# Squares of the last attention's queries on ScalarE, and the moving operands of the products at 64 bytes past multiples of 512

## The chip, the core and the metric

The kernel runs as one program on one core of a Trainium2 chip. The core has five engines that run side by side and meet through semaphores: TensorE (PE in the profile; its weight loads are shown as PEld), VectorE (DVE), ScalarE (ACT), GpSimd (POOL) and SyncE (SP), which issues the DMAs here. The metric is the time of one execution on the device in microseconds, from start to end. On-chip memory (SBUF) has 128 partitions; an address in it, below, is the byte offset of a tile inside each partition, the same in all of them.

## What is computed

The reference runs three transformer blocks on one sequence of 256 tokens and 1024 channels, all in float32. Cut to what matters:

```
x = first_block(x, mem, ...)        # norm, gated mixing + forgetting attention + memory attention, norm, relu^2 FFN
for i in range(2):                  # second block, two layers
    x = x + 0.5 * swiglu(rmsnorm(x, ffn_norm1[i]), wg1, wu1, wd1)   # 1024 -> 2816 -> 1024
    h = rmsnorm(x, mix_norm[i])
    x = x + (sliding_window_attention if i == 0 else latent_attention)(h, ...)
    x = x + 0.5 * swiglu(rmsnorm(x, ffn_norm2[i]), wg2, wu2, wd2)

def latent_attention(h, ...):       # the last attention: 16 heads of 64 + 32 channels
    c_q, c_kv, k_rope = split(h @ w_in)
    q = (rmsnorm(c_q) @ w_uq).reshape(16 heads, 96)
    k, v = from rmsnorm(c_kv) @ w_ukv, k_rope shared by all heads
    q, k = rmsnorm(q) * q_gain, rmsnorm(k) * k_gain      # over the 96 channels of a head
    q, k = rotate the last 32 channels by position
    o = softmax(causal(q k^T / sqrt(96))) v ;  return o @ w_out
```

The norm of a query needs the sum of the squares of its 96 channels; those squares are the first subject of the change.

## The kernel before

**Products.** Activations lie with channels on the partitions and the 256 tokens along the free axis: `x`, and its two parts `xh` and `xl`, are eight tiles of 128 x 256 floats each (1024 bytes per partition). Each float32 product is made of three: value and weight are split into a rounded float32r part and the rest (`h`, `lo`), and `mm_t` (lines 129 to 137) issues for each 128 channels the three matmuls weight-h by value-h (L135), weight-h by value-l (L136) and weight-l by value-h (L137). In `mm_t` the 128 x 128 piece of weights is the stationary operand, and the 128 x 256 activation tile is the one that moves through the array. So each of these matmuls streams 256 columns of an activation tile. `mm_n` (L145 to L147) and `mm_y` (L159 to L161) do it the other way round: activations stationary, weights moving.

The activation tiles that move in `mm_t` are `xh`, `xl` (the normalised residual; gate and up products and most projections), `ah`, `al` (the inner values of the four SwiGLU layers, for the down products), `oh`, `ol` (the attention's output, for its output projection) and `mh`, `ml` (the memory).

**Weights.** They come in as `raw` chunks by DMA from SP's queue, three chunks ahead. ScalarE casts each part to `wh` (L103), VectorE takes the difference to `wl` (L113), six parts deep and four ahead of the products (`Stream`).

**Where tiles lie.** Pools are placed one after another in the order in which they are opened (`lead`, `wp`, `lead2`, `res`, `tp`, `cst`, `sm`, then the pools of each stage), and each tile takes its size rounded up to 32 bytes. A tile without a use therefore moves all that comes behind it. `lead2` begins with one such tile of 8 floats, `fill` (line 172). The addresses of the built program, as remainders by 512 bytes, are:

```
operand                         remainder by 512 bytes
xh, xl  (pool res)              0
ah, al, oh, ol, mh, ml, ch, cl  480   (pools of the stages, behind sm)
wh, wl  (pool wp)               224   (every 128-column piece too)
```

**The last attention.** Queries come in four groups of four heads (`q_mm(0)` to `q_mm(3)`), each as two halves of 128 tokens in the tiles `qn[0]`, `qn[1]`. `q_sq(b)` squares group b into two tiles `qsq` of 128 x 384: group 0 on ScalarE (L1225), groups 1 to 3 on GpSimd (L1223). `q_norm(b)` sums them on VectorE (L1229) and takes the power -1/2 on GpSimd (L198); `q_rope(b)` rotates the last 32 channels (L1240, L1243, L1245), groups 0 and 1 on VectorE, 2 and 3 on GpSimd. `head(h)` transposes a head's keys and queries on TensorE (L1268, L1270) and copies them to `kT` and `qT` (L1273, L1274).

The heads then go through a software pipeline: each `pipe.step()` issues the scores of a new head (L311), the masked maximum and the negated bound of it on VectorE (L1255, L1260), the exponential on ScalarE (L281), the scaling of the head before by its sum on VectorE (L299), the transposes of the one before that (L322, copied by L325) and the products with the values (L343). The code runs under a manual schedule: every engine executes its instructions in the order in which the Python code issues them. So the order of the calls at the end of that stage (`q_mm(1)`, `q_norm(0)`, `head(0, act)`, ...) is the order on each engine, and an instruction that waits holds up all behind it on its engine.

## Time and profile before

| | |
|---|---|
| median of 3 runs | 1250.59 us (1250.11 to 1250.6) |
| the profiled execution: time | 1250.49 us |
| its span, first to last instruction | 1248.7 us |
| mean granted TensorE clock | 0.993 of full speed |
| PE busy / DVE / ACT / POOL | 98% / 67% / 53% / 14% |
| matmuls | 9850 |

A matmul's shown duration (0.28 us for 256 columns) overlaps that of the next: they are pipelined, and a new one starts every 0.12 us or so. What a matmul costs is this distance from start to start, which the timeline shows, and which a stretch of nothing but such matmuls gives as its length by their number. A row of the view by windows counts every matmul that touches the window, so also the two or three that were running when it began.

### The profile page before, as it was taken

To read this page: it belongs to the slowest core of one execution; us is meant where nothing else is said; L and a number is where in the kernel's file an instruction comes from. 1 tells how busy PE (TensorE), PEld (TensorE's weight loads), DVE (VectorE), ACT (ScalarE), POOL (GpSimd) and SP (SyncE) were. 2 spreads that over 40 slices of the span, in tenths; PEclk is the share of its full clock that TensorE was granted. 3 is DMA by queue.
4 is the path that set the end of the run, shared out by engine and by line. 5 is a ranking of instruction groups with operands and counts; after the bars stand their busy time and mean duration, and the time that the engine had idled before them with its cause. 6 is when DMAs were issued, how large, how long until landed. Compare 5 with 4: busy or idle time off the path is not lost.

```text
span 1248.7 us, 23875 instructions
## 1 busy us (share of the span) xinstructions
PE 1222.7 (98%) x9850; PEld 1169.1 (94%) x9850; DVE 836.3 (67%) x1470; ACT 658.8 (53%) x1164; POOL 171.6 (14%) x168
## 2 busy tenths in 40 slices
PE   8998999999999999999999999999999899999998
PEld 6886999888999999988999999999999779999998
DVE  5867776844688666797666666676666797566653
ACT  5574655443554444587454444444444787454532
POOL 5404100300301001212000011000011552000000
PEclk9999999999999999999999999999999989999999
DMA  7543354655254545623455456455455413455462
GB/s 242 200 141 120 130 208 174 234 204 196 75 203 169 181 147 184 233 102 111 168 195 188 143 185 228 173 187 196 146 186 198 169 36 124 161 189 197 137 212 97
DMA packets 37262, 211.31 MB, mean 169 GB/s; under 512 B 4768, under 2 KB 8224, under 8 KB 18848
## 3 DMA queue, kind: packets, MB, share of 16 engines
q1 hardware_dynamic: 37152, 209.78, 48.4%
q8 instruction: 77, 1.26, 0.4%
q14 instruction: 33, 0.27, 0.1%
HBM read 208.71 MB, written 1.05 MB: 168 GB/s over the span
## 4 chain that ended last, share of the span: by engine, by line
PE 84%; DVE 10%; ACT 3%; issue 1%; DMA 1%; POOL 1%; SPq 0%; ACTq 0%; DVEq 0%; POOLq 0%
PE ps L135 23%; PE ps L136 23%; PE ps L137 23%; DVE wl L113 4%; PE ps L161 3%; PE ps L159 3%; PE ps L160 3%; PE ps L343 1%; PE ps L311 1%; PE ps L145 1%; PE ps L147 1%; PE ps L322 1%; PE ps L146 1%; ACT wh L103 1%; DVE p L299 1%
## 5 line engine op out<-in xcount | busy, mean ns | idle before, releaser
L113 DVE TENSOR_TENSOR wl<-raw,wh 128x1024 fp32r<-128x1024 f32 (+4 forms) x436 | 493.0, 1170 | 54.5 <-ACT wh L103 54.2
L135 PE MATMUL ps<-xh,wh 128*128 128x256 f32 (+1 forms) x1848 | 519.9, 281 | 2.2 <-DVE y L527 1.7
L137 PE MATMUL ps<-xh,wl 128*128 128x256 f32 (+1 forms) x1848 | 516.2, 279 | 1.3 <-DVE wl L113 1.3
L136 PE MATMUL ps<-xl,wh 128*128 128x256 f32 (+1 forms) x1848 | 515.9, 279 | 0.3 <-DVE xl L271 0.3
L103 ACT CAST wh<-raw 128x1024 fp32r<-128x1024 f32 (+4 forms) x436 | 400.8, 958 | 94.0 <-PE ps L160 33.9
L135 PEld LDWEIGHTS ps<-xh,wh 128*128 128x128 f32 (+1 forms) x1848 | 346.7, 188 | 5.0 <-ACT sq L208 2.1
L137 PEld LDWEIGHTS ps<-xh,wl 128*128 128x128 f32 (+1 forms) x1848 | 346.6, 188 | 1.8 <-DVE wl L113 1.7
L136 PEld LDWEIGHTS ps<-xl,wh 128*128 128x128 f32 (+1 forms) x1848 | 346.8, 188 | 0.7 <-DVE xl L271 0.5
L135 PE MATMUL ps<-ah,wh 128*128 128x256 f32 x704 | 199.2, 283 | 0.0
L136 PE MATMUL ps<-al,wh 128*128 128x256 f32 x704 | 199.2, 283 | 0.0
L137 PE MATMUL ps<-ah,wl 128*128 128x256 f32 x704 | 199.2, 283 | 0.0
L409 ACT ACTIVATE s<-t 128x256 f32<-128x256 f32 x88 | 36.9, 420 | 187.5 <-DVE t L407 187.5
L137 PEld LDWEIGHTS ps<-ah,wl 128*128 128x128 f32 x704 | 135.2, 192 | 0.0
L136 PEld LDWEIGHTS ps<-al,wh 128*128 128x128 f32 x704 | 135.1, 192 | 0.0
L135 PEld LDWEIGHTS ps<-ah,wh 128*128 128x128 f32 x704 | 135.1, 192 | 0.0
L209 POOL TENSOR_TENSOR acc<-acc,sq 128x256 f32<-128x256 f32 x49 | 54.8, 1119 | 522.2 <-ACT sq L208 521.8
L262 ACT ACTIVATE xh<-x,cols 128x256 fp32r<-128x256 f32 x56 | 28.5, 510 | 111.1 <-DVE x L455 99.1
L223 DVE TENSOR_TENSOR al<-f,ah 128x256 fp32r<-128x256 f32 (+1 forms) x104 | 48.9, 470 | 52.7 <-ACT ah L222 52.7
L407 DVE TENSOR_TENSOR t<-ps,rb 128x256 f32<-128x256 f32 x88 | 37.2, 423 | 69.8 <-PE ps L137 63.1
L222 ACT CAST ah<-f 128x256 fp32r<-128x256 f32 (+1 forms) x104 | 45.8, 440 | 56.6 <-DVE f L411 43.3
L454 DVE SCALAR_TENSOR_TENSOR t<-ps,rb 128x256 f32<-128x256 f32 x32 | 13.6, 425 | 84.4 <-PE ps L137 84.4
L411 DVE TENSOR_TENSOR f<-ps,s 128x256 f32<-128x256 f32 x88 | 37.4, 426 | 47.6 <-ACT s L409 47.6
(270 smaller groups left out, 1411.6 us busy)
## 6 DMA issues: line engine op xcount, KB each, us to landing
raw<-in_gu SPq DMA_DIRECT2D x88, 1024.0 KB, 4.8
raw<-in_dn SPq DMA_DIRECT2D x64, 704.0 KB, 4.4
raw<-in_ff SPq DMA_DIRECT2D x32, 1024.0 KB, 4.9
raw<-in_w_out SPq DMA_DIRECT2D x4, 1024.0 KB, 4.9
raw<-in_aq SPq DMA_DIRECT2D x4, 1024.0 KB, 4.9
raw<-in_a_out SPq DMA_DIRECT2D x4, 1024.0 KB, 5.3
raw<-in_b_out SPq DMA_DIRECT2D x4, 1024.0 KB, 5.1
raw<-in_w1q SPq DMA_DIRECT2D x6, 512.0 KB, 4.4
```

The lines of the kernel that those rows point to most:

```text
L103: act.copy(h[:, :n], t)
L113: eng.tensor_tensor(out=lo, in0=t, in1=h.bitcast(F32), op=ALU.subtract)
L135: pe.matmul(ps, lhsT=h[:, c:c + m], rhs=x[0][k], start=s0, stop=False)
L136: pe.matmul(ps, lhsT=h[:, c:c + m], rhs=x[1][k], start=False, stop=False)
L137: pe.matmul(ps, lhsT=lo[:, c:c + m], rhs=x[0][k], start=False, stop=s1)
L159: pe.matmul(ps, lhsT=x[0][k][:, ts], rhs=h[:, c:c + n], start=s0, stop=False)
L160: pe.matmul(ps, lhsT=x[1][k][:, ts], rhs=h[:, c:c + n], start=False, stop=False)
L161: pe.matmul(ps, lhsT=x[0][k][:, ts], rhs=lo[:, c:c + n], start=False, stop=s1)
L209: gp.tensor_tensor(out=acc, in0=acc, in1=sq, op=ALU.add)
L222: act.copy(h, src)
L223: dve.tensor_tensor(out=lo, in0=src, in1=h.bitcast(F32), op=ALU.subtract)
L411: dve.tensor_tensor(out=f, in0=u, in1=s, op=ALU.mult)
```

## The change

Two edits. First, an unused tile of 24 floats in place of 8 at the head of `lead2`, and a new unused tile of 8 floats, `rest`, at the end of `cst`. All that lies behind `fill` moves by 64 bytes, and all that lies behind `cst` by 96. Of the operands of the products this leaves the weights where they are and puts the others here:

```
operand                         remainder before    after
xh, xl                          0                   64
ah, al, oh, ol, mh, ml, ch, cl  480                 64
wh, wl                          224                 224
```

Second, in the last attention `q_sq` runs on ScalarE for all four groups, and the calls are in another order: the squares of groups 1 and 2, the second half of the values (`v_mm(1)`) and the rotation of group 1 change places with a step of the pipeline.

```diff
     mhalf = lead.tile([P, 24], F32, name="mhalf")
-    lead2.tile([P, 8], F32, name="fill")
+    lead2.tile([P, 24], F32, name="fill")
     rbd = lead2.tile([P, 3, 64], BF16, name="rbd")
...
     posn = cst.tile([P, 2], I32, name="posn")
+    cst.tile([P, 8], F32, name="rest")
...
             for tt, sq in enumerate(qq[b]):
-                qh = qn[tt][:, 4 * b:4 * b + 4, :]
-                if b:
-                    gp.tensor_tensor(out=sq, in0=qh, in1=qh, op=ALU.mult)
-                else:
-                    act.activation(out=sq, in_=qh, func=AF.Square)
+                act.activation(out=sq, in_=qn[tt][:, 4 * b:4 * b + 4, :], func=AF.Square)
...
         head(0, act)
-        q_sq(1)
         q_mm(2)
-        q_sq(2)
         head(1, act)
         head(2, act)
         pipe.step()
         k_rstd(1, ks1)
         head(3, act)
+        v_mm(1)
+        q_sq(1)
+        pipe.step()
         q_rope(1)
-        v_mm(1)
-        pipe.step()
+        q_sq(2)
         pipe.step()
         head(4)
```

TensorE's and SyncE's instructions stand in the same order as before. GpSimd loses its six squares and keeps the rest in order. On the other two engines the first place is ScalarE between the cast of part 354 of the weights and the second transposed head. In the rows, `vb` are the values, `p` the exponentials of a head, `pt` a transposed head. Before:

```order
L103 CAST wh354_12273<-raw183_11958 128x1024
L1286 ACTIVATE vb0_11848<-ps_12276,rv_11990 128x512
L1286 ACTIVATE vb1_11849<-ps_12281,rv_11990 128x512
L281 ACTIVATE p_12300,den_12299<-s_12289,nm_12291,rqb_11867 128x128
L281 ACTIVATE p_12300,den_12299<-s_12289,nm_12291,rqb_11867 128x256
L325 COPY pt_12311<-ps_12307 128x384
L281 ACTIVATE p_12324,den_12323<-s_12313,nm_12315,rqb_11867 128x128
```

And of the change, the same place:

```order
L103 CAST wh354_12256<-raw183_11959 128x1024
L1283 ACTIVATE vb0_11849<-ps_12259,rv_11991 128x512
L1283 ACTIVATE vb1_11850<-ps_12264,rv_11991 128x512
L1222 ACTIVATE qsq_12269<-qn0_11845 128x384
L1222 ACTIVATE qsq_12270<-qn1_11846 128x384
L282 ACTIVATE p_12287,den_12286<-s_12276,nm_12278,rqb_11868 128x128
L282 ACTIVATE p_12287,den_12286<-s_12276,nm_12278,rqb_11868 128x256
L1222 ACTIVATE qsq_12301<-qn0_11845 128x384
L1222 ACTIVATE qsq_12302<-qn1_11846 128x384
L326 COPY pt_12312<-ps_12308 128x384
L282 ACTIVATE p_12325,den_12324<-s_12314,nm_12316,rqb_11868 128x128
```

Two squares now stand ahead of the second head's exponential, and two behind it. The last two of the six stand further down, behind the exponential that follows `k_scale(1)`.

The second place is VectorE at the same time: the masked maximum of the second head (`s`, `mx`), the scaling of the first (`p`), and the rotation of query group 1 (`rt`, `qn0`, `qn1`). Before:

```order
L113 TENSOR_TENSOR wl353_12192<-raw182_11880,wh353_12191 128x1024
L1240 TENSOR_TENSOR rt_12263<-qn0_11844,tq_113 128x4x16
L1240 TENSOR_TENSOR rt_12264<-qn1_11845,tq_113 128x4x16
L1243 TENSOR_TENSOR qn0_11844<-qn0_11844,tq_113 128x4x32
L1245 TENSOR_TENSOR qn0_11844<-qn0_11844,rt_12263 128x4x32
L1255 ISA s_12289,mx_12290<-ps_12236,kmask_111 128x128
L1260 SCALAR_TENSOR_TENSOR nm_12291<-mx_12290,rqb_11867 128x2
L299 TENSOR_SCALAR p_12246<-p_12246,rd_12292 128x128
L113 TENSOR_TENSOR wl354_12274<-raw183_11958,wh354_12273 128x1024
```

And of the change:

```order
L113 TENSOR_TENSOR wl353_12189<-raw182_11881,wh353_12188 128x1024
L1252 ISA s_12276,mx_12277<-ps_12229,kmask_111 128x128
L1257 SCALAR_TENSOR_TENSOR nm_12278<-mx_12277,rqb_11868 128x2
L300 TENSOR_SCALAR p_12239<-p_12239,rd_12279 128x128
L113 TENSOR_TENSOR wl354_12257<-raw183_11959,wh354_12256 128x1024
L1237 TENSOR_TENSOR rt_12291<-qn0_11845,tq_113 128x4x16
L1237 TENSOR_TENSOR rt_12292<-qn1_11846,tq_113 128x4x16
L1240 TENSOR_TENSOR qn0_11845<-qn0_11845,tq_113 128x4x32
L1242 TENSOR_TENSOR qn0_11845<-qn0_11845,rt_12291 128x4x32
```

The rotation of group 1, eight instructions in all, now stands behind the second head's maximum, the first head's scaling and one weight difference.

## Rows read from the trace of the kernel before

**Rows 1.** The page: busy time by engine, and the chain by engine.
```profile
PE 1222.7 (98%) x9850; PEld 1169.1 (94%) x9850; DVE 836.3 (67%) x1470; ACT 658.8 (53%) x1164; POOL 171.6 (14%) x168
...
PE 84%; DVE 10%; ACT 3%; issue 1%; DMA 1%; POOL 1%; SPq 0%; ACTq 0%; DVEq 0%; POOLq 0%
```

**Rows 2.** TensorE's groups by line and shape: count, busy us, mean ns, idle.
```profile
L135 PE MATMUL ps<-xh,wh 128*128 128x256 f32 x1840 | 517.7, 281 | 2.2 <-DVE y L527 1.7 <-ACT rb L255 0.5
...
L135 PE MATMUL ps<-ah,wh 128*128 128x256 f32 x704 | 199.2, 283 | 0.0
...
L135 PE MATMUL ps<-oh,wh 128*128 128x256 f32 x128 | 37.5, 293 | 0.0
...
L135 PE MATMUL ps<-mh,wh 128*128 128x256 f32 x16 | 4.7, 293 | 0.0
...
L135 PE MATMUL ps<-xh,wh 128*32 128x256 f32 x8 | 2.2, 280 | 0.0
```

**Rows 3.** Windows: length; busy and count of PE, PEld, DVE, ACT, POOL; clock; DMA.
```profile
620.00:710.00 90.00, 90.00 (x774) 90.00 (x773) 56.58 (x81) 43.52 (x65) 0.00 (x0) 1.00 0.52 181
715.00:775.00 60.00, 60.00 (x502) 60.00 (x501) 38.96 (x55) 29.57 (x47) 7.78 (x6) 1.00 0.56 189
...
905.00:960.00 55.00, 55.00 (x460) 55.00 (x460) 34.45 (x50) 25.05 (x43) 7.62 (x6) 1.00 0.57 189
230.00:310.00 80.00, 80.00 (x355) 66.26 (x354) 46.45 (x41) 31.56 (x33) 8.57 (x6) 1.00 0.60 212
```

**Rows 4.** Timeline of a down product: start us, duration us, engine, line, operands.
```profile
759.77 0.28 PE L135 MATMUL ps<-ah,wh 128*128 128x256 f32 x1
...
762.89 0.28 PE L137 MATMUL ps<-ah,wl 128*128 128x256 f32 x1
```

**Rows 5.** Windows in the last attention, columns as in rows 3.
```profile
990.00:995.00 5.00, 5.00 (x34) 4.44 (x33) 3.88 (x10) 3.87 (x12) 4.50 (x3) 1.00 0.60 210
995.00:1000.00 5.00, 2.14 (x12) 1.35 (x11) 5.00 (x18) 3.67 (x9) 5.00 (x4) 0.93 0.61 210
1000.00:1005.00 5.00, 5.00 (x27) 4.81 (x26) 4.96 (x22) 4.30 (x13) 1.68 (x2) 0.73 0.01 3
```

**Rows 6.** Timeline there, PE: in brackets idle time before, and what ended it.
```profile
999.44 0.87 PE L322 MATMUL ps<-kon,p 128*128 128x128 f32 x3 [2.76 <-DVE p L299]
```

**Rows 7.** Timeline there, POOL: squares of groups 1 and 2, then of 3.
```profile
993.03 4.23 POOL L1223 TENSOR_TENSOR qsq<-qn 128x384 f32<-128x384 f32 x4
...
1010.30 2.06 POOL L1223 TENSOR_TENSOR qsq<-qn 128x384 f32<-128x384 f32 x2
```

**Rows 8.** Timeline there, DVE: rotations of groups 0 and 1, scalings of heads.
```profile
986.95 0.62 DVE L1240 TENSOR_TENSOR rt<-qn,tq 128x64 f32<-128x64 f32 x4
...
994.92 2.59 DVE L1240 TENSOR_TENSOR rt<-qn,tq 128x64 f32<-128x64 f32 x4
...
1004.02 0.55 DVE L299 TENSOR_SCALAR p<-p,rd 128x128 f32<-128x128 f32 x2
...
1011.55 1.23 DVE L299 TENSOR_SCALAR p<-p,rd 128x128 f32<-128x128 f32 x2
```

**Rows 9.** Timeline there, ACT: the squares of group 0, and exponentials that waited.
```profile
985.52 0.97 ACT L1225 ACTIVATE qsq<-qn 128x384 f32<-128x384 f32 x2
...
999.12 0.49 ACT L281 ACTIVATE p<-s,nm,rqb 128x128 f32<-128x128 f32 x1 [1.33 <-DVE nm L1260]
...
1001.47 0.49 ACT L281 ACTIVATE p<-s,nm,rqb 128x128 f32<-128x128 f32 x1 [0.65 <-DVE nm L1260]
...
1011.73 0.49 ACT L281 ACTIVATE p<-s,nm,rqb 128x128 f32<-128x128 f32 x1 [1.63 <-DVE nm L1260]
```

## The prediction

> **What bounds the kernel now.** I read the page first: PE is busy 98% of the span, and the chain that ended last lies 84% on it [rows 1]. So TensorE sets the time, and the question is what one matmul costs. The groups by line and shape give the counts: nearly all matmuls stream 256 columns of an activation tile [rows 2]. The shown durations (281 and 283 ns) overlap and don't price them; the windows do. In a gate-and-up stretch, where `xh` and `xl` move, 774 matmuls touch 90 us; one lasts 0.28 us, so about 2.4 of them had begun earlier, and 90 / 771.6 is 116.6 ns from start to start. In down stretches, where `ah` and `al` move, it is 60 / 499.7 and 55 / 457.7, 120.1 and 120.2 ns [rows 3]; the timeline there shows 26 starts in 3.12 us, 120.0 ns each [rows 4]. PE, PEld, clock (1.00) and count are gapless in both, and DVE, ACT and DMA have room (56.58 and 43.52 of 90 us, a DMA share of 0.52 [rows 3]). Two families of equal matmuls on the same weights thus differ by 3.4 ns, and what is known to differ is where the moving tile lies: remainder 0 by 512 bytes for x, 480 for the others.
>
> The stretch with 512 moving columns gives 80 / 353.3 = 226.4 ns [rows 3]. From 256 to 512 columns that is 106.4 ns more, so 256 columns cost 106.4 and a fixed part is left: 13.6 ns at remainder 480, 10.2 at 0.
>
> The other place that the change touches is the last attention. PE stands still there for 2.76 us before a transpose that waits for VectorE's scaling [rows 6], and behind it the clock is at its lower level (1.2 of 2.4 GHz) for part of two windows, 0.93 and 0.73 [rows 5].
>
> **The change part by part.** *Tiles that go from 480 to 64.* `ah`, `oh` and `mh` move in 704 + 128 + 16 = 848 groups of three matmuls [rows 2], 2544 in all. No row shows a moving tile at remainder 64. Bounds: no loss is shown beyond the 13.6 ns that these have already, so 0 gained; at the other end the fixed part is gone, 2544 x 13.6 = 34.6 us gained. I take the value of the nearest known place: 64 lies nearer to 0 than to 480, and like 0 it is a multiple of 64, which 480 and 224 are not. That makes 3.4 ns each: 2544 x 3.4 = 8.6 us gained. All of it is on the path, since PE runs without gaps in the down stretches; about 1.3 us of it (the 384 of `oh`) is in attention stages, where other engines may take some back.
>
> *`xh` and `xl` from 0 to 64.* They move in 1840 + 8 groups, 5544 matmuls. By the same choice nothing changes. Bounds: with the fixed part of 480 they lose 5544 x 3.4 = 18.8 us; with none they gain 5544 x 10.2 = 56.5 us.
>
> *Stationary activations* (`mm_n`, `mm_y`: some 740 matmuls) move too, while the weights that move in them stay at 224. The two kinds of stationary tile stand in no clean pair of rows; taken as 0, bounds plus and minus 3.4 ns, 2.5 us.
>
> *Constants and scratch* (`tp`, `cst`, `sm` and what VectorE, ScalarE and GpSimd read) move by 64 or 96 bytes: taken as 0. These engines hide behind PE in the long stretches; an error of 1% of VectorE's 56.58 us in 90 still leaves it a third of the time free.
>
> *GpSimd's squares.* 4.23 us for groups 1 and 2 and 2.06 for group 3 [rows 7] go. GpSimd is not on the path, but what runs beside it on VectorE is: the four small products of the rotation took 0.62 us in group 0 and 2.59 in group 1, under GpSimd's squares; a head's scaling took 1.23 in place of 0.55 under the squares of group 3 [rows 8]. That is 1.97 and 0.68 us of VectorE given back.
>
> *The rotation of group 1* moves behind the second head's maximum and the first head's scaling. The scaling, for which PE waited 2.76 us, then comes about 3.3 us sooner (the rotation's length with its later parts), so this wait is gone, and with it the reason for the lower clock behind it: (0.07 + 0.27) x 5 = 1.7 us of PE's time at 1.2 GHz [rows 5]. Late next is the query transpose of head 4, which waits for the rotation, and ScalarE.
>
> *Squares on ScalarE.* Six more, 0.97 us for a pair [rows 9], 2.9 us. The first two pairs, 1.94 us, fill idle time that stood there: 1.33 + 0.65 = 1.98 us before two exponentials [rows 9]. So ScalarE reaches the cast and the query copies behind them when it did before; what PE gained by then it waits off again for these copies. Queued behind the squares are the exponential, the transposed head's copy and the next cast; PE waits for each. The last pair follows an exponential that had waited 1.63 us for VectorE [rows 9], which VectorE's 0.68 us pays for in part. Bounds for the whole attention edit: 2.76 + 1.7 = 4.5 us gained if ScalarE holds up nothing, 2.9 lost if all six squares come on top. Between them I take 0.7 us gained, the 0.68 of the scaling, because ScalarE's idle time matches its new work almost exactly.
>
> **The sum.** The profiled execution took 1250.49 us, with a span of 1248.7 and 1.8 around it; the median shown is 1250.59, so the two agree. 1250.5 - 8.6 - 0.7 = 1241.2 us. Its own range is 1236 to 1246, from the attention's bounds and the stationary tiles.
>
> **Rivals.** *Another step down.* From 480 to 0, 32 bytes further on, the fixed part fell by a quarter. If it falls as much again at 64, x gains 5544 x 3.4 = 18.8 us and the rest 2544 x 6.8 = 17.3: 1250.5 - 36.1 - 0.7 = 1213.7 us; by two steps, 37.7 + 25.9, 1186 us. For it: 10.2 ns are still there to lose, and VectorE and DMA have the room. Against: two points make no line, and no row of 256 columns in this stretch form goes under 116.6.
>
> *Only 0 is good.* What helps x could be that it starts on a multiple of 512 (or 128 or 256). Then 64 is as bad as 480: the 5544 matmuls of x take 120.0 ns, 18.8 us more, the other 2544 gain nothing, and the time is 1250.5 + 18.8 - 0.7 = 1268.6 us. It decides as soon as x's step rises above 116.6 + 8.6 / 5544, that is 118.2 ns. For it: the only family with the short step is the only one at 0. Against: the matmuls of 512 columns at 224 have the same fixed part as those at 480, so the remainder by 512 as such is not what counts; 224 and 480 share only their remainders by 256 and less.
>
> *The place doesn't matter.* The families could differ for another reason (which tiles they come from, what else runs), and each keeps its step. Then only the attention edit is left: 1249.8 us. For it: no row shows the same tile at two places. Against: `oh` is written by ScalarE and VectorE as x is, and sits at 283 or more like `ah` [rows 2]. [...]
>
> **How the numbers follow.** The forecast 0.42; another step down 0.30, a third of it below 1200; only 0 is good 0.17, with half steps in it; the place doesn't matter 0.11. A measurement of this kernel tells about 0.2%, 2.5 us, from no change. Faster: 0.42 + 0.30 + 0.01 = 0.73; within 0.2%: 0.10 from the last case; slower 0.17. The range from 1195 to 1262 leaves out the lowest of the first rival and the full price of the second, about 0.2 together.
>
> **What would show it.** In the profile after, the down stretches should show some 516 matmuls in 60 us (116.6 ns) and the gate-and-up stretches still 774 in 90. 795 in 90 (113.2) for x would be the first rival, 752 the second; 502 in 60 for the down products with 774 for x, the third. In the attention the wait of 2.76 us for L299 should be gone, the rotation of group 1 should take 0.6 us for its four products, and the exponentials' idle time of 1.33 and 0.65 should be filled by squares. The forecast is wrong if x's step moves at all by more than half a ns, or if the attention stage differs by more than 3 us from before.

## The result, and the profile after

The changed kernel takes 1266.68 us (median of 4 runs, 1265.6 to 1267.12), the kernel before 1250.35 in the same series; the ratio is 1.0129, 95% interval 1.0117 to 1.0142. So it is slower by 16.3 us, where 1241.2 us was forecast, and the time lies outside the range that went up to 1262. The profiled execution took 1267.12 us, its span 1265.3. Of the executions behind the times below one is left out: one of the four of `addr_only` ran at 0.556 of the full clock and took 1979 us.

The page of the kernel after, busy time by engine and the chain by engine. PE still sets the time, and its share of the chain has grown [rows 1]:

```profile
PE 1241.3 (98%) x9850; PEld 1186.1 (94%) x9850; DVE 834.0 (66%) x1470; ACT 660.0 (52%) x1170; POOL 166.7 (13%) x162
...
PE 89%; DVE 6%; ACT 3%; issue 1%; DMA 1%; POOL 0%; SPq 0%; DVEq 0%; ACTq 0%; POOLq 0%
```

The same windows as in [rows 3], of the kernel after (length; busy and count of PE, PEld, DVE, ACT, POOL; clock; DMA):

```profile
620.00:710.00 90.00, 90.00 (x753) 90.00 (x752) 56.24 (x80) 42.80 (x63) 0.00 (x0) 1.00 0.53 188
715.00:775.00 60.00, 60.00 (x502) 60.00 (x501) 35.97 (x53) 26.70 (x46) 4.94 (x4) 1.00 0.52 172
...
230.00:310.00 80.00, 80.00 (x344) 64.29 (x343) 46.05 (x41) 33.04 (x35) 12.21 (x8) 1.00 0.57 200
```

The gate-and-up window held 774 matmuls and now holds 753: 90 / 750.6 = 119.9 ns from start to start, where it was 116.6. The down window has 502 as before. The window with 512 moving columns went from 355 to 344, 226.4 to 80 / 342.3 = 233.7 ns. In the gate-and-up window the clock, VectorE, ScalarE and the DMA are as they were, so none of them shows a reason for the longer step.

If every matmul's step to the next one is summed by family over both traces, the whole difference is placed. The rows are worked out from the start times of all PE instructions, in us, with the count:

```
family                                count   before    after
x moves (256 columns)                  5544   656.44   674.72   +18.3
ah, al move (256 columns)              2111   253.29   253.32     0.0
weights move under ah, al (512)         384    87.08    89.96    +2.9
no weights: transposes, scores, sums   1018   111.72   109.89    -1.8
attention: query products (384)          48     9.55     8.59    -1.0
first products of the program (390)      48    15.44    13.91    -1.5
all others                              696   109.70   109.50    -0.2
sum                                           1243.2   1259.9   +16.7
```

The 1.5 us of the first products lie at the program's start and say nothing of the change: in the profiles of the kernels below this family takes 15.4 or 13.9 us, whatever differs elsewhere.

In the last attention, the timelines of the kernel after (start us, duration us, engine, line, names, shapes; in brackets idle before and what ended it). On VectorE the four small products of the rotation of group 1 and the scaling that had taken 1.23 us, then squares and exponentials on ScalarE:

```profile
1013.09 0.63 DVE L1237 TENSOR_TENSOR rt<-qn,tq 128x64 f32<-128x64 f32 x4
...
1025.63 0.68 DVE L300 TENSOR_SCALAR p<-p,rd 128x128 f32<-128x128 f32 x2
```

```profile
1009.19 0.49 ACT L282 ACTIVATE p<-s,nm,rqb 128x128 f32<-128x128 f32 x1 [0.67 <-DVE nm L1257]
...
1012.97 0.93 ACT L1222 ACTIVATE qsq<-qn 128x384 f32<-128x384 f32 x2
...
1013.80 0.49 ACT L282 ACTIVATE p<-s,nm,rqb 128x128 f32<-128x128 f32 x1
```

The four products take 0.63 us where they took 2.59, the scaling 0.68 where it took 1.23 [rows 8], and the exponential behind the squares no longer waits. What PE waits for there, first in the kernel before, then after (line waited for: us in all, times, longest; the three largest):

```profile
PE ps L322 <- DVE p L299: 3.2, 2, 2.8
PE ps L1268 <- DVE kc L1209: 2.1, 3, 0.8
PE ps L1270 <- DVE qn L1245: 0.9, 1, 0.9
```

```profile
PE ps L1267 <- DVE qn L1242: 2.8, 2, 1.9
PE ps L1265 <- DVE kc L1210: 1.8, 3, 0.7
PE ps L312 <- ACT qT L1271: 1.7, 2, 1.1
```

The wait of 2.8 us for the scaling is gone, and others of the same sum have come: 6.2 us before, 6.3 after. But none is longer than 1.9 us, and the clock does not fall. It was granted at 0.93 and 0.73 in two windows of 5 us before [rows 5], and again at 0.80 and 0.86 in two windows from 1010 us on; first these two, then the same stretch of the program after, at 1.00:

```profile
1010.00:1015.00 5.00, 3.87 (x20) 2.17 (x21) 5.00 (x19) 3.32 (x11) 5.00 (x11) 0.80 0.00 0
1015.00:1020.00 5.00, 5.00 (x34) 4.00 (x34) 4.20 (x21) 3.95 (x13) 1.88 (x2) 0.86 0.00 0
```

```profile
1025.00:1030.00 5.00, 4.63 (x33) 3.36 (x33) 4.96 (x24) 4.20 (x14) 3.33 (x9) 1.00 0.00 0
1030.00:1035.00 5.00, 4.20 (x33) 3.52 (x34) 4.00 (x24) 4.99 (x18) 1.03 (x1) 1.00 0.01 2
```

### The profile page after: what moved, and what is told of

It reads as the page before. It is cut to its first block, busy times and chain, and to the rows that moved or that the text cites. A ratio compares the mean times of both kernels' runs of the same rounds, so it can differ in the third digit from the quotient of the medians.

```text
span 1265.3 us, 23880 instructions
## 1 busy us (share of the span) xinstructions
PE 1241.3 (98%) x9850; PEld 1186.1 (94%) x9850; DVE 834.0 (66%) x1470; ACT 660.0 (52%) x1170; POOL 166.7 (13%) x162
## 4 chain that ended last, share of the span: by engine, by line
PE 89%; DVE 6%; ACT 3%; issue 1%; DMA 1%; POOL 0%; SPq 0%; DVEq 0%; ACTq 0%; POOLq 0%
PE ps L137 25%; PE ps L135 25%; PE ps L136 24%; PE ps L161 3%; PE ps L159 3%; PE ps L160 3%; DVE wl L113 2%; PE ps L312 1%; PE ps L344 1%; PE ps L323 1%; PE ps L145 1%; PE ps L147 1%; PE ps L146 1%; ACT p L282 1%; ACT wh L103 1%
## 5 line engine op out<-in xcount | busy, mean ns | idle before, releaser
L135 PE MATMUL ps<-xh,wh 128*128 128x256 f32 (+1 forms) x1848 | 525.7, 284 | 2.2 <-DVE y L528 1.7
L137 PE MATMUL ps<-xh,wl 128*128 128x256 f32 (+1 forms) x1848 | 523.4, 283 | 2.7 <-DVE wl L113 2.7
L135 PEld LDWEIGHTS ps<-ah,wh 128*128 128x128 f32 x704 | 132.2, 188 | 0.0
L137 PEld LDWEIGHTS ps<-ah,wl 128*128 128x128 f32 x704 | 131.6, 187 | 0.0
```

The costliest lines, as they stand in the source:

```text
L135: pe.matmul(ps, lhsT=h[:, c:c + m], rhs=x[0][k], start=s0, stop=False)
L137: pe.matmul(ps, lhsT=lo[:, c:c + m], rhs=x[0][k], start=False, stop=s1)
```

## The experiments

**One half at a time.** `addr_only` has the two pads and the attention of before, `att_only` the attention edit and the places of before.

> Only the two pads: every tile of the products at 64 past a multiple of 512 bytes, attention as before. Theory S (the place of the moving tile sets the step, 116.7 ns at remainder 0, 120.0 at any other seen so far): the 5544 matmuls of xh and xl cost 3.3 ns more each, 18.5 us, the others nothing; 1250.4 + 18.5 = 1268.9 us (1267.5 to 1270), and 753 matmuls in a gate-and-up window of 90 us. Rival T (the changed attention is what loses, through tiles that are late): about 1250 us, 774 in 90. Rival H (both lose): between 1255 and 1265.

> Only the attention edit: squares on ScalarE, the rotation of group 1 later; all places as before. Theory S: what is left of the measured +16.3 us after 18.5 is -2.2, so 1248.1 us (1247 to 1249.5), no lower clock behind the transposes of head 3. Rival T: 1253 us or more. My own forecast gave 0.7 us gained, 1249.7.

Measured: `addr_only` 1269.0 us (ratio 1.0148, 1.0132 to 1.0163), `att_only` 1248.55 us (0.9984, 0.9975 to 0.9993). The two add up to the whole: +18.6 - 1.9 = +16.7, measured +16.3. So the pads lose, the attention gains a little, and x at 64 is as slow as `ah` at 480. The windows of `addr_only`:

```profile
620.00:710.00 90.00, 90.00 (x753) 90.00 (x752) 56.29 (x79) 43.16 (x64) 0.00 (x0) 1.00 0.54 189
715.00:775.00 60.00, 60.00 (x502) 60.00 (x501) 36.35 (x54) 26.16 (x44) 4.93 (x4) 1.00 0.52 176
```

**All tiles at 0.** If 0 were simply good, `ah` should gain there.

```diff
     posn = cst.tile([P, 2], I32, name="posn")
+    cst.tile([P, 8], F32, name="rest")
```

> First pad left at 8 columns, second pad added: ah, al, oh, ol, mh, ml go from remainder 480 to 0, xh and xl stay at 0; attention as before. Theory S: 2544 matmuls gain 3.3 ns each, 8.5 us: 1241.9 us (1241 to 1243), 514 matmuls in a down window of 60 us. Rival F (the two families differ for another reason than their place): 1250.4 us, 502 in 60.

Measured: 1247.39 us (0.997, 0.9959 to 0.9981). `ah` does gain what was expected, 516 matmuls in the down window, but the time gains only 3.0 of 8.5 us. The missing part shows in the window of 512 columns, where the *weights* move, at 224 as ever, and only the stationary tile has gone from 480 to 0:

```profile
715.00:775.00 60.00, 60.00 (x516) 60.00 (x515) 39.94 (x56) 29.78 (x48) 7.75 (x6) 1.00 0.59 197
...
230.00:310.00 80.00, 80.00 (x345) 64.41 (x344) 45.60 (x40) 31.57 (x33) 8.71 (x6) 1.00 0.59 210
```

80 / 343.3 = 233.0 ns, where it was 226.4. That is 6.6 ns for 480 products, 3.2 us, and with it the sum is -5.3, which is what the profiled execution shows (span 1243.5 for 1248.7 us); it is the fastest of the six, and their median lies 2 us above it. So the moving tile's own place can't be all: theory S, the reading held until then, fails here.

**A staircase.** `xh` and `xl` are laid out in pairs with 64 bytes between the pairs.

```diff
+    xh, xl = [], []
+    for k in range(KT):
+        xh.append(res.tile([P, T], F32R, name=f"xh{k}"))
+        xl.append(res.tile([P, T], F32R, name=f"xl{k}"))
+        if k < KT - 1:
+            res.tile([P, 16], F32, name=f"pad{k}")
```

> xh_k and xl_k at 64 x k past a multiple of 512 bytes, k = 0 to 7; ah and the rest at 416. Theory S in its strict form (only remainder 0 is short): 116.7 ns for the three matmuls of k = 0, 120.0 for each other k, mean 119.6; the time about 1250.4 + 5544 x 7/8 x 3.3 = 16.2, 1266.6 us. Rival M (short at each multiple of 256): k = 4 short too, 1264.3 us. Rival N (short at each multiple of 128): k = 0, 2, 4, 6 short, 1259.6 us. In each ah at 416 stays at 120.0.

Measured, in one execution: 1254.79 us, under all three. By tile (mean of 40 chains, in units of 1/2.4 ns, called cycles here and below: 288 of them are 120.0 ns) k = 0 to 3 took 290.8, 286.1, 286.6, 281.4 and k = 4 to 7 took 287.2, 286.1, 286.7, 281.3: but for the first tile of a chain the pattern repeats after 256 bytes. No tile shows the 280 of x before, though k = 0 and 4 stand at the same distance from the weights, so a tile's step depends on its neighbours too, and a staircase can't price single places. Two other families fell out of it: `ah`, now at 416, took 282.7 cycles, a step not seen before, and a family of 256 moving columns of weights (at 224, with the memory tile at 416 as the stationary one) took 272.

**A table of pairs.** A kernel that only issues matmuls, in the order of products of `mm_t`, with the stationary tile at s and the moving one at m.

```diff
+            pe.matmul(ps[:, :n], lhsT=st[:, c:c + w], rhs=mv[:, d:d + n], start=i == 0, stop=i == count - 1)
```

> A kernel that computes nothing of the reference: it only issues groups of matmuls between a stationary buffer and a moving buffer, in the order of products of the kernel, each group with one pair of places (moving at m, stationary at s past a multiple of 512 bytes; 256 columns, m in steps of 32 up to 480, s in steps of 32 up to 224; then 512 columns, m and s up to 224). Theory S (the moving tile's place alone): the step of 256 columns is 280 cycles of 2.4 GHz for m = 0, about 283 for 416, 288 for 64 and 480, the same for every s, and 512 columns at m = 224 take 544 whatever s is. Theory P (the pair decides, since 512 columns at m = 224 took 544 with s = 480, 549 with s = 416, 560 with s = 0 and 562 with s = 64 in the full kernels, and 256 columns at m = 224 with s = 416 took 272): the step changes with s at one m, repeats after 256 bytes, and the pairs seen so far come out as in the full kernels: (0, 224) 280, (64, 224) 288, (224, 224) 288, (160, 224) 283, (224, 160) 272. Rival E (what VectorE, ScalarE and the DMA do beside it makes the difference): all pairs take the same here.

Measured (mean step of the last 24 or 12 matmuls of a group, from the start times, in the same cycles; four of the 16 rows of m for 256 columns, three of the 8 for 512):

```
256 columns    s =   0     32     64     96    128    160    192    224
m =   0          288.0  284.0  272.0  288.0  285.1  288.0  282.6  282.7
m =  32          282.7  287.7  284.0  272.0  288.0  285.2  288.0  282.7
m =  64          282.6  282.7  288.0  284.0  272.0  288.0  285.2  288.0
m = 256          288.0  284.0  272.0  288.0  285.2  288.0  282.7  282.7

512 columns    s =   0     32     64     96    128    160    192    224
m =   0          550.4  560.0  560.0  562.0  560.0  560.0  549.4  560.0
m =  32          560.0  544.0  560.0  560.0  562.2  560.0  560.0  549.4
m = 224          559.4  560.0  561.0  558.0  560.0  549.2  560.0  546.4
```

The values run along diagonals: what counts is the *distance*, stationary place minus moving place, by 256 bytes. There is next to nothing beside PE in this kernel (VectorE and ScalarE are busy 1% of its span, the DMA queues took 0.7%) and the steps differ all the same, so rival E is out. The known steps fit: x before was at distance 224 (280 cycles in the kernel, 280 or 282.7 here), x after at 160 (288), `ah` at 0 before and 160 after (288 and 288), the 512 columns at 0 (544), 32 when all tiles lay at 0 (560) and 96 after (562). But one distance can have two steps: in the row of m = 96, not shown, distance 192 gave 272, and elsewhere 282.7.

**The distance in the kernel.** `w_moved` is `addr_only` with the weights moved by the same 64 bytes; `x32` has x at 32 and the rest at 0.

```diff
     mhalf = lead.tile([P, 24], F32, name="mhalf")
+    lead.tile([P, 16], F32, name="shift")
```

> All activation tiles at 64 as in the changed kernel, but the split weights moved by the same 64 bytes, from 224 to 288; attention as before. Distance is taken as stationary place minus moving place, by 256 bytes. Theory P (the distance decides): xh and xl see 224 as in the kernel before, 280 cycles a step; ah and al see 224 too, 280 instead of 288; the 480 products with 512 columns see 32 and take 560 in place of 544. 1250.4 - 2544 x 3.3 + 480 x 6.7 = 1245.2 us (1243 to 1247), 774 matmuls in 90 us and 516 in 60. Theory S (the place of the moving tile decides, and 64 is bad): 1269 us as with the two pads alone, 753 and 502.

> The first pad at 16 columns: xh and xl at 32, all tiles behind them at 0, weights at 224, attention as before. Theory P: x sees distance 192, for which the table showed 272 cycles in two of its groups and 282.7 in the others; ah sees 224, 280 cycles; 512 columns see 32, 560. So 1250.4 - 8.5 + 3.2 = 1245.1 us plus either 5544 x -3.3 = -18.5 (1226.6 us) or 5544 x 1.1 = +6.2 (1251.3 us); which of the two depends on how the stream falls into step, and a mean between them if it falls into both. Theory S: x is no longer at 0, so 120.0 ns: 1250.4 + 18.5 - 8.5 + 3.2 = 1263.6 us.

Measured: `w_moved` 1246.56 us (0.9965, 0.9955 to 0.9976), 22 us less than `addr_only`, with the activations at the very same places. `x32` 1247.2 us (0.9978, 0.9967 to 0.999); in its profiled execution (1249.26 us) x went at 282.7 cycles in every long stretch, 766 in 90 us. Theory P had 1251.3 us for that step, 4 us more than the median, and this rest is not explained; theory S had 1263.6. The windows of `w_moved`:

```profile
620.00:710.00 90.00, 90.00 (x774) 90.00 (x773) 57.11 (x81) 43.18 (x64) 0.00 (x0) 1.00 0.52 181
715.00:775.00 60.00, 60.00 (x517) 60.00 (x516) 38.22 (x56) 28.62 (x47) 7.75 (x6) 1.00 0.58 194
...
230.00:310.00 80.00, 80.00 (x344) 64.43 (x343) 46.02 (x39) 31.65 (x34) 10.66 (x7) 1.00 0.59 208
```

64 gives 774 again once the weights are at 288. This settles the sign of the result: the distance between the two tiles was changed, from a good one to a bad one.

**More than one step at a distance.**

> Computes nothing of the reference: groups of 60 matmuls of 256 columns, order of products as in the kernel, eight distances (stationary minus moving place, by 256 bytes, steps of 32), each ten times behind a short group with another column count, so that the stream enters at ten different moments; then the same with the two weight parts at different places, and with the two activation parts at different places. Theory P1 (one step per distance): all ten entries of a distance agree within 0.3 cycles: 288 at 0, 284 at 32, 272 at 64, 288 at 96, 285 at 128, 288 at 160, 282.7 at 192 and 224. Theory P2 (a distance has more than one steady step, and the entry picks it): 64 and 192 show both 272 and 282.7, 224 shows 280 and 282.7, and 0, 96 and 160 stay at 288 whatever the entry.

Measured, ten entries each (mean of the last 36 matmuls): 288.0 at distances 0 and 160 every time, 283.7 to 284.3 at 32; 272.0 nine times and 282.7 once at 64, and the same at 192; 281.5 to 285.0 at 96; 284.7 to 288.0 at 128; 280.0 four times and 282.7 six times at 224. So P2 holds at 64, 192 and 224: a stream falls into one of two steps and keeps it. At 96, where P2 had 288 whatever the entry, it failed. (With the two weight parts, or the two activation parts, at different distances no pair other than 64 with 64 or 192 went under 277.)

**The two halves of the attention edit.** `att_squares` has the squares on ScalarE in the order of before, `att_order` the new order with the squares on GpSimd.

> Squares of all groups on ScalarE, order of before: ScalarE's new 1.94 us stand before the exponential of head 1 and in front of the next cast. Theory O (the later rotation is what shortens the wait for head 3's scaling, the squares only take GpSimd off VectorE): 1249.5 to 1250.5 us, wait of 2 us or more left at L299, a stretch at half clock left. Theory Q (GpSimd's squares are what stretched the rotation: 2.59 for 0.62 us): the four products take 0.6 us, the wait falls under 1 us, clock 1.00 all through, 1248.5 us.

> The new order with the squares of groups 1 to 3 still on GpSimd. Theory O: 1248.5 us as the whole attention edit, clock 1.00 all through. Theory Q: no gain, 1250.4 us, since the rotation still meets GpSimd's squares and the norm of group 1 waits for them.

Measured: `att_squares` 1248.47 us (0.9987, 0.9978 to 0.9996), `att_order` 1251.13 us (1.0007, 0.9998 to 1.0016). The time is theory Q's: the gain is the squares', through VectorE, whose four products took 0.6 us in `att_squares` too, and with them the wait for the scaling went.

The stage itself says so more plainly than the whole time does. In the profiled executions, from its first product on `ch` to its last with the values, it took 66.1 us before, 66.4 in `att_order`, 63.2 in `att_squares`, 63.7 in `att_only` and 63.8 in the change: 2.3 to 2.9 us gained with the squares on ScalarE, nothing by the order. In the whole time this mixes with x's two steps at distance 224: its 5544 matmuls took 656.4 us before, 659.2 in `att_only` and 659.5 in `att_squares`, where the gate-and-up window holds 767 matmuls and not 774:

```profile
620.00:710.00 90.00, 90.00 (x767) 90.00 (x766) 56.45 (x80) 43.17 (x64) 0.00 (x0) 1.00 0.51 180
```

Q's clock of 1.00 all through did not come, it was 0.70 in one window of `att_squares`:

```profile
1010.00:1015.00 5.00, 3.71 (x19) 2.58 (x19) 5.00 (x21) 3.18 (x11) 3.44 (x8) 0.70 0.10 41
```

With the order alone PE waits longer, now for the rotation, and the clock is at half, 0.50, behind the wait. The waits of `att_order`, then a window of it:

```profile
PE ps L1270 <- DVE qn L1245: 5.1, 2, 4.1
PE ps L1268 <- DVE kc L1209: 1.3, 2, 0.7
```

```profile
1000.00:1005.00 5.00, 4.40 (x15) 4.24 (x16) 4.97 (x25) 2.84 (x7) 1.51 (x1) 0.50 0.02 3
```

**Each family at its own distance.** `split_zero` puts the moving tiles of the later layers at 0 by a pad at the head of their pools, and leaves the tiles under 512 columns at 480. `kick192` goes for 272 at distance 192.

```diff
+            fa.tile([P, 8], F32, name="lift")
             ah = [fa.tile([P, T], F32R, name=f"ah{j}") for j in range(22)]
```

> The attention edit; xh and xl at 0 as before; the tiles that move in the down and output products of the later stages (ah and al of the gated layers, oh and ol of the last two attentions) at 0, distance 224; the tiles that are stationary under 512 moving columns (first layer's ah, al, oh, ol) left at 480, distance 0. Theory P: 2496 matmuls from 288 to 280 cycles, -8.3 us, the 480 products with 512 columns keep 544, and the attention edit -1.9: 1250.4 - 10.2 = 1240.2 us (1239 to 1242). Theory S (place of the moving tile): the same -8.3 and the same 1240.2; the two differ in the window of 512 columns, where S leaves no reason why all tiles at 0 lost 3.2 us there; 353 to 355 matmuls in 80 us by P as before.

> As the version before in the attention, but moving tiles at distance 192 (x, ah, oh at 32, weights at 224; the tiles under 512 columns at 224, distance 0), and every 120 matmuls or so one matmul of 144 columns more, whose result the next one overwrites: it shifts the moment at which the stream goes on, as the short groups in the entry table did, which led to 272 cycles nine times in ten. Theory P2 (the entry picks the step and nothing else does): 8040 matmuls near 272 cycles, 1250.4 - 18.5 - 16.6 - 1.9 + 5 for some 65 added matmuls = 1218 us (1214 to 1226). Rival C (in the full kernel the other engines' traffic or the chains of 24 hold the stream at 282.7): 1250.4 + 6.2 - 5.6 - 1.9 + 5 = 1254 us.

Measured: `split_zero` 1242.81 us (0.9944, 0.9932 to 0.9956), 774, 517 and 355 matmuls in the three windows: all families at the better of the distances tried so far, 2.6 us above the expected sum and outside its range. In its profiled execution 1224 matmuls of x, in three stretches outside these windows, went at 282.7, some 1.4 us of it. `kick192` 1253.98 us (1.0028, 1.0018 to 1.0038), rival C's number: in the long stretches x and `ah` went at 282.7, but for some 70 matmuls of x that went at 272.0 behind a wait of PE at 150.6 us, until the next added matmul. P2 had not said which disturbance changes the step, and the added matmul led to 272 nowhere.

**What holds a stream at 282.7.** Three more kernels of nothing but matmuls: `place_apart` tries the kernel's own layout above 256 bytes and its chains of 24, `place_traffic` the work of the other engines beside the stream, `place_kick` a narrower matmul in it.

> Computes nothing of the reference: chains of 24 matmuls of 256 columns as in the kernel, three chains behind each short group, distances 0 to 480 in steps of 32 (stationary minus moving place, now by 512), two entries each, in four layouts: the second weight part 4096 bytes behind the first and the second activation part 8192 behind the first, as in the kernel; one or the other or both 512 bytes further, as both were in the entry table. Rival A (the layout within 1024 bytes decides between 272 and 282.7 at distances 64 and 192): the kernel's layout stays at 282.7 at 64, 192, 320 and 448 for all entries, and the layout with both 512 further shows 272. Rival C (the other engines' traffic in the full kernel decides): all four layouts show 272 at 64 and 192 for most entries. Rival B (chains of 24 instead of 60): all four show 282.7.

> Computes nothing of the reference: at each of the distances 192, 64 and 224 six phases of 288 matmuls (some 33 us), in each of them first nothing beside them, then casts of 1024 columns on ScalarE (24 times 0.96 us), then subtractions of 1024 columns on VectorE (20 times 1.17 us), both, transfers of 1 MB (six), and all three. Rival C (the other engines' traffic holds the kernel's stream at 282.7): 272 cycles at 192 and 64 with nothing beside, 282.7 from some point on under one kind of traffic or more, and not back after it. Theory P2 as it was (the entry alone): every phase as it entered, 272 in most, with no change within a phase.

> Computes nothing of the reference: at distances 192 (entered from nine matmuls at distance 160, and without them) and 64 (entered from nine at 32) 24 to 26 matmuls of 256 columns, one of n columns (n from 32 to 248 in steps of 8), and 24 more. Theory P2 (the moment at which the stream goes on picks the step): some n take a stream at 282.7 to 272 and some the other way, by ranges of n; then an added matmul of the right width would free the full kernel. Rival L (a stream that has fallen into a step keeps it across a matmul of any width): the 24 behind go as the 24 ahead in all 252 trials.

Measured: in `place_apart` all four layouts agree within 0.2 cycles, 272.0 at 64 and 192 in each entry, and distances 256 apart give the same, so layout and chain length are out. In `place_traffic` every phase kept one step from its second chain on: 282.7 at 192 and 272.0 at 64 in all six phases. At 224 the phase with nothing beside it went at 280.1 and the five with traffic at 282.7; but the first of these five was at 282.7 already in its first chain, over at 478.30 us, before its first cast began at 478.39, so here too the entry had chosen. Its windows, at 192 alone and with all traffic, then at 64 alone and with all traffic:

```profile
40.00:60.00 20.00, 20.00 (x172) 20.00 (x171) 0.00 (x0) 0.00 (x0) 0.00 (x0) 1.00 0.00 1
...
208.00:228.00 20.00, 20.00 (x172) 20.00 (x171) 19.09 (x21) 18.94 (x21) 0.00 (x0) 1.00 0.78 316
240.00:260.00 20.00, 20.00 (x179) 20.00 (x178) 0.00 (x0) 0.00 (x0) 0.00 (x0) 1.00 0.00 1
410.00:430.00 20.00, 20.00 (x179) 20.00 (x178) 19.24 (x21) 19.09 (x21) 0.00 (x0) 1.00 0.77 315
```

172 and 179 matmuls stand unchanged beside transfers of over 300 GB/s and a VectorE and ScalarE that are busy 19 of 20 us: rival C's cause, traffic, is out as far as these three go. In `place_kick` the nine matmuls at distance 32 led into 272 in all 84 trials at distance 64; one narrower matmul then threw 69 of them to 282.7 (those of 112, 192, 200, 208 and 224 columns did not), while at 192 all 168 stayed at 282.7. So neither P2's easy form nor L: the step depends on what runs just before, and the fast one can be lost to a single matmul. That the slow one is harder to leave would be more than this shows, for the two were tried at different distances.

**Distance 64 in the kernel.** `at64` has x at 160 and the later layers' tiles at 416, those under 512 columns at 224, weights at 224, and the attention edit. `kick64` adds the nine matmuls at 32.

```diff
-    lead2.tile([P, 8], F32, name="fill")
+    lead2.tile([P, 48], F32, name="fill")
...
+    cst.tile([P, 24], F32, name="rest")
...
+            fa.tile([P, 48], F32, name="lift")
```

> The attention edit; every moving activation tile of 256 columns at distance 64 (weights at 224, x at 160, the later layers' tiles at 416), the tiles under 512 columns at 224, distance 0; no added matmul. If the fast step is lost at the first stall or narrower matmul and never comes back by itself: 282.7 cycles for all 8040, 1250.4 + 6.2 - 5.6 - 1.9 = 1249 us. If the kernel's entries lead to 272: 1250.4 - 18.5 - 16.7 - 1.9 = 1213 us.

> The same places, and ahead of a chain nine matmuls more with the stationary slice 32 bytes back (distance 32), whose result is overwritten: whenever the products change between x and another tile, and every 960 matmuls. If the entry decides (from a distance of 32 into 64 all streams of the last table went at 272): some 20 kicks of 1.06 us cost 21 us, the 8040 matmuls give 35 back against the kernel before, 1250.4 - 35 - 1.9 + 21 = 1234 us, 794 matmuls in a gate-and-up window of 90 us. If something of the kernel itself (waits for weights, chains that alternate between banks) throws the stream back to 282.7: 1249 + 21 = 1270 us, 764 in 90.

> The same kernel as at64, timed against the kernel before. If the streams fall into 272 cycles in every execution, as in the profile: 1221 us (1220 to 1224), ratio 0.976 to 0.978. If the step varies from execution to execution: single times up to 1249 us.

Measured: `at64` 1221.49 us in one execution and, as `at64_timed`, 1220.87 us (1219.69 to 1223.54), ratio 0.9763, 0.975 to 0.9777: between the two times expected, 29.5 us less than before and 46 less than the change. `kick64` 1235.94 us (0.9879, 0.9862 to 0.9895); its 162 added matmuls, some 19 us, win 4 back. The kernel's own entries lead into 272 in most streams, so the kicks aren't needed. Windows of `at64_timed` (its stages lie earlier by 15 us):

```profile
605.00:695.00 90.00, 90.00 (x796) 90.00 (x796) 59.78 (x85) 46.37 (x68) 0.00 (x0) 1.00 0.56 195
700.00:760.00 60.00, 60.00 (x532) 60.00 (x531) 38.21 (x56) 27.31 (x47) 6.38 (x5) 1.00 0.59 200
230.00:310.00 80.00, 80.00 (x355) 66.26 (x354) 46.58 (x41) 32.69 (x35) 11.15 (x7) 1.00 0.59 210
```

```profile
178.00:200.00 22.00, 22.00 (x189) 22.00 (x188) 14.01 (x16) 11.86 (x16) 0.00 (x0) 1.00 0.54 191
```

796 in 90 us is 113.4 ns, 272 cycles. The last row is a stretch of x in the first layer that went at 22 / 186.6 = 117.9 ns, 283 cycles, in the same execution and at the same distance; counted in sixes, some 3950 of the 5544 matmuls of x took the fast step in this profile and 4190 in the other.

What changes the step in a full kernel can be read from the traces. In the twelve with x at distance 224, 192 or 64, wherever a stream of x, `ah` or `oh` changed midway between lasting steps, without a new shape or an added matmul, PE had waited. Two such waits, of `at64` and then of `at64_timed` (start us, duration us, in brackets the wait):

```profile
586.52 0.38 PE L136 MATMUL ps<-xl,wh 128*128 128x256 f32 x1 [0.53 <-DVE xl L272]
```

```profile
152.24 0.38 PE L137 MATMUL ps<-xh,wl 128*128 128x256 f32 x1 [0.36 <-DVE wl L113]
```

The first took x from 282.6 to 272.0 cycles, the second from 272.0 to 282.7, so the slow step can be left too. The length of the wait alone does not choose: with 0.45 us from start to start at 151 us, x kept 280.0 in the kernel before and went on at 282.6 in `split_zero`.

## Why the prediction was wrong

**What bounds the kernel** was right: PE, and the price of one matmul. The two steps, 116.6 and 120.1 ns, were read rightly, and so were the counts; the 5544 steps of x decided the result.

**The step that failed** is the sentence "what is known to differ is where the moving tile lies". The two families differed in that, but also in the distance to their stationary tile, 224 against 0, and the weights at 224 stood beside the moving places in the same list. `w_moved` is the test that parts them: same moving places as `addr_only`, x's step back at 116.7, 22 us between the two. From this one reading follow the wrong terms: "64 lies nearer to 0 than to 480" gave 8.6 us gained for `ah`, `oh` and `mh`, measured 0; "by the same choice nothing changes" for x, measured +18.3, the lost end of the bounds that the prediction had put there (18.8) and left for the rival.

**Stationary activations**, taken as 0 with bounds of 2.5 us for 740 matmuls: the 384 of the first layer alone cost 2.9, 7.5 ns each. The bound was made from the 3.4 ns between two moving places, and at 512 columns the pair moves the step by more.

**Constants and scratch** cost nothing: over the whole program a weight difference of 1024 columns took 1278 ns on VectorE before and 1277 after, a cast on ScalarE 958 both times, and `addr_only` is explained without them.

**The attention edit** went as told in its first half: 1.96 us of rotation and 0.55 of the 0.68 us of scaling given back on VectorE, the wait of 2.76 us gone, the clock at 1.00. The size was off, 1.9 us gained and not 0.7, within the bounds of -4.5 and +2.9. The sum of PE's waits stayed, as forecast, though in shorter pieces: 1.7 us of them are now for ScalarE's query copies, which the prediction had named. What it left out is the clock. It counted the lower clock of two windows (1.7 us by its formula) and not of the two at 0.80 and 0.86 (again 1.7, an estimate in the same way), and both stretches went. What it writes as 1.2 GHz is in the trace of the kernel before a granted share of 0.50, from 999.32 to 1002.73 us, and under it the products of 384 columns start every 320 ns, 1.2 columns per ns; just behind, at 1.00, every 173 to 175. Its 2.4 is the rate between 256 and 512 columns at 1.00, both pairs of tiles a multiple of 256 bytes apart: 256 columns more took 106.3 ns (120.1 to 226.4). It also put the lower clock down to the wait of 2.76 us, but the second stretch began behind waits of no more than 0.8 us. That the squares carry the gain and the moved rotation nothing, `att_squares` and `att_order` showed; the prediction had credited the order with the end of the wait.

**The rivals.** "Only 0 is good" gave 1268.6 us, near the measured time, but by luck, for its reason is wrong too: 64 is as good as 0 with the weights at 288 (774 matmuls in 90 us, `w_moved`), and x at 160 is better than either (796, `at64_timed`). The distance 160 that the change made happens to cost the 288 cycles of distance 0. The argument against it, that 512 columns at 224 have the fixed part of 480, was no reading: the subtraction of one stretch from the other had put it in. Still it held the answer: with 480 moving and 224 stationary, or the other way round, the two are 256 apart, distance 0, the slowest for 256 columns (288 cycles) and the fastest for 512 in the kernel (544). "Another step down" was right that x could go faster, at another distance and not at another place of its own; of the 10.2 ns that it saw, `at64` took 3.3 (its sign, 795 in 90 us, left out the two or three matmuls already running: at 113.2 ns it is 797). "The place doesn't matter" fell with x's step, 116.6 ns before and 119.9 after, and with the table's 272 to 288 cycles for one pair of buffers.

**Open.** What lets the clock fall in one attention and not in the other was not settled. Which of its two steps a stream takes behind a wait was not found. Why `ah` at distance 64 went at 282.7 in `stairs64` and at 272 in `at64` was not tried apart; that the stretch of x ahead of it sets the entry is an argument from the tables. What in the chip makes the distance count was not seen either: the trace has starts of weight loads and matmuls, not their reads.

## What to carry to other kernels

Two families of equal matmuls with different steps are a find, but before one cause is charged, list everything in which they differ, here also the place of the other operand; then ask which third family (512 columns) the cause would have to explain as well. Where a price hangs on one such reading, the range should reach its other bound in full. And place the tiles of a matmul as pairs: hold the weights fixed, choose each activation tile's distance from them by the shape it is used in, and look at the count of matmuls in a long window to see which step it fell into.

## What the runs showed that was not expected

- The step of a 256-column matmul, on float32r operands and with other weights each time, ran from 272 to 288 cycles (113.3 to 120.0 ns) by the distance between stationary and moving tile modulo 256 bytes; of a 512-column one from 544 to 562. The best distances differ: 64 or 192 for 256 columns (272), 0 for 512 (544.0 to 550.4 in the rows shown, 549.2 to 549.4 at 192); in the full kernels 272 lasted at 64, while at 192 only some 80 matmuls behind waits took it.
- At one distance a stream can have two lasting steps (272 and 282.7 at 64 and 192, 280 and 282.7 at 224), chosen by what ran just ahead, and a wait of PE can change it in either direction; work on VectorE and ScalarE (19 of 20 us busy) and on DMA (316 GB/s) did not change the step of any phase in `place_traffic`.
- In the last attention the clock stood at its lower level, 0.50, behind waits of PE of 2.8 us (before) and 4.1 us (`att_order`), and stayed at the upper one, 1.00, through waits of up to 1.9 us after. The longest wait alone does not tell it, though: before, it fell a second time, to windows of 0.80 and 0.86, behind waits of 0.8 us at most, and in `att_squares`, where none was longer than 1.2 us, it was 0.70 in one window.
